# Sums of squares of the norms: elementwise adds on VectorE and GpSimd and one-column products instead of products with ones

## The chip, the cores and the metric

The kernel runs on one core of a Trainium2 chip. The metric is the device time of one execution in microseconds, from repeated runs. TensorE (PE in the profile; its weight loads are PEld) multiplies matrices into PSUM, VectorE (DVE), ScalarE (ACT) and GpSimd (POOL) work elementwise, and SyncE (SP) issues the transfers. Each engine takes its instructions in a fixed order and waits on semaphores for the others.

## What is computed

One inference step of a hybrid flow-matching model: two layers over 512 latent tokens and 128 context tokens of 1024 features, all in float32. A layer, cut to what matters here:

```python
def rmsnorm(x, g):
    y = x * rsqrt(mean(x * x, axis=-1, keepdims=True) + 1e-6)
    return y * g

h = rmsnorm(x, g_pre1) * (1 + scale1) + shift1
y = concat(diff_attention(h), gqa(h), ssd(h), s5(h)) @ w_out     # h @ w_in feeds all four
x = x + gate1 * rmsnorm(y, g_post1)
h = rmsnorm(x, g_pre2) * (1 + scale2) + shift2
g, v = split(dwconv(h @ w_up))
x = x + gate2 * rmsnorm((silu(g) * v) @ w_down, g_post2)
```

Every sub-block thus has a norm over 1024 features before and after it. The SSD mixer ends with a norm over 256 features, and queries and keys are normed over 64.

## The kernel before

Activations lie with features on the 128 partitions and tokens along the columns: a tensor of 1024 features is eight chunks of 128 x 642 (512 latent columns, two of padding, 128 context columns). The big products are done in float32 as three passes over a high and a low part of weights and activations (`lin3`, line 124), so a chunk of weights costs three instructions on TensorE per group of columns. Weights come through a pair of raw tiles `wr` (line 94); ScalarE casts the high part (line 103), VectorE and GpSimd take turns at the subtraction for the low part (line 106).

The tokens are worked in two groups, `SPANS` (line 48): columns 0 to 256 and 256 to 642. Around each norm the second group's products are meant to run on TensorE while the first group's norm is done. The functions that matter:

- `square` (line 305) is called once per chunk. ScalarE squares the chunk's columns into a tile `nsq` (line 311), and TensorE multiplies it by 32 columns of ones, which adds up the 128 features of the chunk (line 313). Chunk `c` writes into the quarter `c % 4` of the rows of a PSUM tile, so two chunks are added up in each quarter.
- `rstd` (line 315) is called once per group. ScalarE copies the four partial sums to `nsb` (line 322). For each tile of 128 tokens a one-column product with `sel4` adds the quarters and puts the tokens on the partitions (line 324). `rsqrt` (line 295) is one VectorE operation (line 300) and one power on GpSimd (line 302). A product with the identity broadcasts the factors over the partitions again (line 327).
- `prenorm` (line 334) makes the next activations from x (lines 345 to 353). `postnorm` (line 355) adds the normed y to x, chunk by chunk (VectorE line 365, then VectorE or GpSimd in turn, line 368), and calls `square` on the new x for the prenorm that follows.
- `norms` (line 375) ties the two: the first group's postnorm comes directly, its prenorm is kept back in `pending` until output tile `MID` = 6 of the second group is under way (`between`, line 387).

These norms are met at: the start (squares of x, `start`, line 1533 on); the output projection of each layer (squares of y in `put`, line 1601; of x in `postnorm`); the last block of the down projection of each layer (squares of y, line 1421; of x in `postnorm`, in layer 0 only, for layer 1's first norm). That makes 16 groups of eight squares. The SSD norm (line 1034 on) has two groups of two squares per layer. Behind the output projection come the first tiles of the up projection (`ffn_first`), behind layer 0's down projection the first tiles of layer 1's input projection (`first_proj`); both are worked group by group (`leading`, line 394).

The order of the instructions on an engine is not written by hand: a scheduler places them at build time by priorities (`prio`, with the numbers of `PR`, line 42) and by its own estimate of when things are ready. Tiles of a tag share their buffers: `nsq` has four for the first group, `nsr` two for the second (`NQ`, `NTMP`, lines 31 and 45).

Of the kernel before, what the change touches and what calls it, by code (L numbers as in the profile page):

```python
# [14 lines left out]
P = 128  # L15
# [15 lines left out]
NQ = (4, 2)  # L31
# [13 lines left out]
NTMP = (("nsq", SPLIT, NQ[0]), ("nsr", TW - SPLIT, NQ[1]))  # L45
# [23 lines left out]
for _n, _w in (("ident", 128), ("ones", 128), ("blk64", 2), ("su", 129), ("lt", 129),  # L69
               ("selc", 8), ("selh", 4), ("mhalf", 16), ("sel4", 1)):  # L70
    CST[_n] = (_o, _o + _w)
    _o += _w
# [3 lines left out]
class K:  # L76
# [10 lines left out]
    def load_w(self, src, nk, nm=128, keep=None, parts=None):  # L87
        """weights as (hi, lo) with hi + lo exact; they stay in the pool `keep` if one is given"""
# [20 lines left out]
    def load_w2(self, src, pool):  # L109
        """the same for 8 input chunks, as lists of their parts, in the place of hidden chunks"""  # L110
# [13 lines left out]
    def lin3(self, o, w, xs):  # L124
        """o = w^T x in three passes over the (hi, lo) parts"""
# [23 lines left out]
    def tri(self, lower, strict):  # L149
        """mask of the triangle of the rows not below (or not above) the columns"""  # L150
        o = int(strict == lower)
        return self.c("lt" if lower else "su")[:, o:o + 128]
# [13 lines left out]
    # exact-ish exponential on small tiles: returns (p, s), exp(x) = s * (1 + p)  # L166
# [30 lines left out]
    def cmul(self, pool, dre, dim, ar, ai, br, bi, nm, shp, e1=None, e2=None):  # L197
        """d = a * b on float planes (broadcast APs allowed)"""
# [17 lines left out]
    # ------------------------------------------------------------ adaLN  # L216
# [7 lines left out]
    def adaln(self, l, lo, hi, pool, banks="pp", bufs=2):  # L224
        """groups lo .. hi - 1 of 2048 columns of the modulation, in steps"""
# [16 lines left out]
    def adaln_end(self, l, g, parts, ps, pool, bank, sel, bufs):  # L242
        """column sums to the features on partitions; the 512s of a group lie in the order 0, 2, 1, 3"""
# [14 lines left out]
    def adaln_first(self, pool):  # L258
        """shift and scale of the first norm, half of the features after the other"""
# [12 lines left out]
    def gains(self, l, which):  # L272
        """(1 + scale) * g_pre, gate * g_post for sub-block `which` (0 mixer, 1 FFN)"""
# [20 lines left out]
    # ------------------------------------------------------------ norms  # L294
    def rsqrt(self, pool, ss, n, feats, tag):
        """(ss / feats + EPS) ** -0.5 on a small tile"""
# [8 lines left out]
    def square(self, pool, ps, gi, src, c, n=8, tmp=None):  # L305
        """adds src ** 2 over the features of chunk c of n for one group of tokens to the sums in ps (on the rows of a
        quarter, which depends on the chunk)"""
        t0, t1 = SPANS[gi]
        tmp = tmp or NTMP[gi]
        sq = pool.tile([P, tmp[1]], F32, tag=tmp[0], name="nsq", bufs=tmp[2])[:, :t1 - t0]  # L310
        self.nc.scalar.activation(sq, src[:, t0:t1], AF.Square)
        j = c % 4
        self.mm(ps[32 * j:32 * j + 32, 0:t1 - t0], self.c("ones")[:, 0:32], sq, c < 4, c >= n - 4)

    def rstd(self, pool, ps, gi, feats, tag="n", tmp=None):
        """per token 1 / rms from the sums in ps, on all partitions of ps; a function of the columns"""
        t0, t1 = SPANS[gi]
        tmp = tmp or NTMP[gi]
        n = len(LOC[gi])
        m = min(feats // 4, P)  # L320
        sb = pool.tile([P, tmp[1]], F32, tag=tmp[0], name="nsb", bufs=tmp[2])
        self.nc.scalar.copy(sb[0:m, 0:t1 - t0], ps[0:m, 0:t1 - t0])
        for j, c in enumerate(LOC[gi]):
            self.mm(ps[:, 400 + j:401 + j], sb[0:m, c - t0:c - t0 + 128], self.c("sel4")[0:m], True, True)
# [9 lines left out]
    def prenorm(self, pool, l, which, gi, acc):  # L334
        """h = rmsnorm(x) * (1 + scale) * g_pre + shift for one group of tokens"""
# [19 lines left out]
    def postnorm(self, pool, l, which, gi, acc, y, nacc, out=None):  # L355
        """x += gate * rmsnorm(y) * g_post for one group of tokens; nacc collects the squares of the new x"""
# [18 lines left out]
    def norms(self, pool, gi, st, y, post, pre, out=None):  # L375
        """from the sums of a group of tokens to the next activations; the end of the first group comes behind the
        start of the second one"""
        nacc = self.pss("ud"[gi])
# [8 lines left out]
    def between(self, m):  # L387
        """the rest of the first group's norms, once output tile MID of the second group is under way"""
# [4 lines left out]
    # ------------------------------------------------------------ input projection tiles  # L393
    def leading(self, jobs, bank, keep, wprio, place=None):
        """several output tiles, one group of the tokens after the other;
        jobs: (weights, put(first column, PSUM)), bank(i): PSUM tile"""
# [11 lines left out]
    def put(self, d, alt=0):  # L408
        """plain evacuation to the columns of a tile"""
# [10 lines left out]
    def dwconv(self, x, w, b, out):  # L420
        """centred depthwise conv of width 3 along the token axis"""
# [6 lines left out]
    def silu2(self, t, out, half):  # L428
        """out = silu(2 * half) by way of t"""
# [3 lines left out]
    def ysplit(self, c, src, scale=None):  # L433
        """mixer output chunk c (sample columns from 0, prompt columns at the end of src) to (hi, lo)"""
# [11 lines left out]
    # ------------------------------------------------------------ S5  # L446
    def first_proj(self, l, pb, lead):
        """inputs of the S5 mixer (columns ordered by position in the chunk of 8, chunk), first queries and keys,
        gates of the SSD"""
# [24 lines left out]
    def s5_tables(self, l, pool, bank="dd", wprio=None, bufs=1):  # L474
        """tables that depend on the parameters alone, to DRAM"""
# [17 lines left out]
        # step sizes, a_bar, input gain  # L493
# [56 lines left out]
        # powers a^0..a^8  # L550
# [6 lines left out]
        # unit phases e^{i theta 8 2^s}, decay |a|^8  # L557
# [13 lines left out]
        # powers per position in the chunk: into the states, out of the states  # L571
# [1205 lines left out]
```

## Time and profile before

| what | value |
|---|---|
| three runs | 2275.59, 2281.47, 2284.01 us; median 2281.47 |
| profiled execution | span 2270.7 us from the first to the last instruction, 32188 instructions |
| TensorE | busy 2064.1 us (91%), mean granted clock 0.930 of full |
| TensorE weight loads | 1692.5 us (75%) |
| VectorE | 1166.1 us (51%) |
| ScalarE | 728.5 us (32%) |
| GpSimd | 706.0 us (31%) |
| transfers | 232.19 MB, mean 102 GB/s |
| the chain that ended last | TensorE 75%, DMA 9%, VectorE 7%, GpSimd 3% |

The page gives the profiled execution's span and no device time of its own beside it; the runs' median lies 10.8 us above the span. Busy time of an engine is the time that its instructions took, with overlaps counted once. TensorE is pipelined: its instructions overlap, so the duration of one is longer than the time that it takes from its neighbours. The clock is granted at one of two levels, 1.2 or 2.4 GHz; 1.00 is the upper one throughout.

### The profile page before, as it was taken

The numbers are of one execution on the slowest core, as the hardware profiler recorded it, in microseconds if no ns is written. First come the engines' busy times: TensorE is split into PE (matmuls) and PEld (weight loads), VectorE is DVE, ScalarE is ACT, GpSimd is POOL, SyncE is SP. The second block draws the span as 40 slices with busy tenths as digits, with TensorE's granted clock in tenths as the row PEclk, the third lists the DMA queues.
The fourth block names the chain that finished last, engine by engine and source line by source line (L and its number), as shares of the span: only waits on it lengthen the run. The fifth ranks groups of instructions, "written<-read, shape, count | busy, mean of one in ns | idle before, by whom it ended". The sixth has DMA issues, their size and how long they took to land.

```text
span 2270.7 us, 32188 instructions
## 1 busy us (share of the span) xinstructions
PE 2064.1 (91%) x12698; PEld 1692.5 (75%) x12698; DVE 1166.1 (51%) x2376; ACT 728.5 (32%) x1256; POOL 706.0 (31%) x747
## 2 busy tenths in 40 slices
PE   5994988899999999999988889887989999999997
PEld 2884753454779788899976877655557899999985
DVE  7864874434558567233335358564565451323343
ACT  3421342232344223223324224343234443323231
POOL 4642523222232344122223324322233231212131
PEclk9996988889999999999998989888988999999998
DMA  7554324314313575422222542321022012222221
GB/s 285 165 179 135 121 68 124 93 49 142 108 38 108 166 247 186 131 82 63 84 77 77 174 131 90 111 67 49 11 65 94 19 47 84 70 80 68 82 75 47
DMA packets 95199, 232.19 MB, mean 102 GB/s; under 512 B 18120, under 2 KB 31816, under 8 KB 95048
## 3 DMA queue, kind: packets, MB, share of 16 engines
q1 hardware_dynamic: 95048, 230.14, 32.0%
q8 instruction: 100, 1.64, 0.3%
q14 instruction: 51, 0.42, 0.1%
HBM read 193.52 MB, written 36.58 MB: 101 GB/s over the span
## 4 chain that ended last, share of the span: by engine, by line
PE 75%; DMA 9%; DVE 7%; POOL 3%; issue 2%; ACT 2%; SPq 2%; POOLq 0%; DVEq 0%; ACTq 0%
PE psb L85 34%; PE psp L85 14%; PE pse L85 9%; PE psv L85 7%; PE psd L85 7%; PE psu L85 2%; DMA wm<-in_w_mod 1%; DMA ck<-in_cache_bk 1%; DMA ck<-in_cache_ak 1%; DMA wr<-in_w_down 1%; DMA s5yd<-s_u 1%; DMA wr<-in_w_out 1%; DMA s_tb<-s5td 1%; DMA s_u<-s5ud 1%; SPq L1160 1%
## 5 line engine op out<-in xcount | busy, mean ns | idle before, releaser
L85 PE MATMUL psb<-hh,wh 128*128 128x256 f32 (+1 forms) x1152 | 358.9, 312 | 2.3 <-DVE cv L425 2.3
L85 PE MATMUL psb<-hl,wh 128*128 128x256 f32 (+1 forms) x1152 | 357.9, 311 | 0.0
L85 PE MATMUL psb<-hh,wl 128*128 128x256 f32 (+1 forms) x1152 | 357.0, 310 | 0.0
L106 POOL TENSOR_TENSOR wl<-wr,wh 128x1024 fp32r<-128x1024 f32 (+3 forms) x83 | 181.6, 2188 | 449.5 <-ACT wh L103 427.1
L103 ACT CAST wh<-wr 128x1024 fp32r<-128x1024 f32 (+3 forms) x166 | 160.4, 966 | 427.9 <-PE psb L85 285.1
L85 PEld LDWEIGHTS psb<-hh,wh 128*128 128x128 f32 x1152 | 217.8, 189 | 13.2 <-issue 8.2
L85 PEld LDWEIGHTS psb<-hl,wh 128*128 128x128 f32 x1152 | 218.5, 190 | 3.4 <-issue 3.4
L85 PEld LDWEIGHTS psb<-hh,wl 128*128 128x128 f32 x1152 | 217.8, 189 | 3.4 <-issue 3.4
L85 PE MATMUL psp<-hh,wh 128*128 128x386 f32 (+1 forms) x544 | 182.2, 335 | 40.2 <-DVE dtr L839 13.1
L106 DVE TENSOR_TENSOR wl<-wr,wh 128x1024 fp32r<-128x1024 f32 (+3 forms) x83 | 95.2, 1147 | 184.5 <-ACT wh L103 184.0
L85 PE MATMUL psp<-hl,wh 128*128 128x386 f32 (+1 forms) x544 | 176.3, 324 | 1.5 <-DVE hl L353 1.4
L85 PE MATMUL psp<-hh,wl 128*128 128x256 f32 (+1 forms) x544 | 175.6, 324 | 0.0
L85 PE MATMUL psb<-uh,wh 128*128 128x256 f32 (+1 forms) x544 | 169.7, 312 | 0.0
L85 PE MATMUL psb<-ul,wh 128*128 128x256 f32 (+1 forms) x544 | 168.9, 310 | 0.0
L85 PE MATMUL psb<-uh,wl 128*128 128x256 f32 (+1 forms) x544 | 168.6, 310 | 0.0
L85 PEld LDWEIGHTS psp<-hh,wh 128*128 128x128 f32 x544 | 109.7, 202 | 52.8 <-DVE dtr L839 13.6
L85 PE MATMUL psv<-at_e,vt 128*64 128x512 f32 x240 | 136.3, 681 | 10.2 <-ACT at_e L1237 10.1
L1377 POOL TENSOR_TENSOR cv<-cv,cv 128x642 f32<-128x642 f32 x44 | 71.3, 1622 | 169.6 <-DVE cv L425 140.2
L85 PE MATMUL pse<-k,q 96*128 96x128 f32 (+5 forms) x288 | 100.2, 407 | 21.9 <-issue 6.7
L424 DVE SCALAR_TENSOR_TENSOR cv<-psb,vec,cv 128x641 f32<-128x641 f32 x72 | 63.4, 881 | 103.3 <-ACT cv L423 103.3
L85 PEld LDWEIGHTS pse<-k,q 96*128 96x128 f32 (+2 forms) x288 | 54.4, 205 | 79.0 <-issue 59.6
L85 PEld LDWEIGHTS psp<-hl,wh 128*128 128x128 f32 x544 | 109.5, 201 | 4.0 <-DVE hl L353 2.5
(497 smaller groups left out, 4596.5 us busy)
## 6 DMA issues: line engine op xcount, KB each, us to landing
wm<-in_w_mod SPq DMA_DIRECT2D x96, 512.0 KB
wr<-in_w_up SPq DMA_DIRECT2D x88, 512.0 KB
wr<-in_w_in SPq DMA_DIRECT2D x30, 512.0 KB
wr<-in_w_down SPq DMA_DIRECT2D x32, 384.0 KB
wr<-in_w_down SPq DMA_DIRECT2D x32, 320.0 KB
wr<-in_w_out SPq DMA_DIRECT2D x16, 512.0 KB
s_tb<-s5td SPq DMA_DIRECT2D x8, 992.0 KB
s_to<-s5td SPq DMA_DIRECT2D x8, 768.0 KB
```

What stands on the lines that cost most here:

```text
L85: self.nc.tensor.matmul(out, w, x, start=start, stop=stop)
L103: nc.scalar.copy(hv, rv)
L106: e.tensor_sub(lv, rv, hv.bitcast(F32))
L424: nc.vector.scalar_tensor_tensor(out[:, 1:TW], x[:, 0:TW - 1], w[:, 0:1], out[:, 1:TW], op0=ALU.mult, op1=ALU.add)
L1160: nc.sync.dma_start(k2[0:64, 0:TW].bitcast(F32), self.qd["bk"][0, r])
L1377: G.tensor_mul(cv[0], cv[0], cv[1])
```

## The change

The products with ones go. `square` still has ScalarE square each chunk. In a norm over 1024 features the squares of chunks 0 and 1 get tiles of their own (`na{gi}{c}`); those of chunks 2, 4 and 6 are added onto the first by VectorE, those of chunks 3 and 5 onto the second by GpSimd, and chunk 7 keeps its tile. `rstd` then has three tiles of squares (two in the SSD norm) and sums each over the features, with the tokens on the partitions, by a product of the tile as the stationary operand with one column of ones; three products are added up in PSUM per 128 tokens. The copy to `nsb` and the constant `sel4` are gone, as is the wait of `square` on PSUM. Both groups share the two buffers of `nsr` for chunks 2 to 7. The rest of the diff empties comments and docstrings.

```diff
-NQ = (4, 2)
-NTMP = (("nsq", SPLIT, NQ[0]), ("nsr", TW - SPLIT, NQ[1]))
+NTMP = (("nsr", TW - SPLIT, 2), ("nsr", TW - SPLIT, 2))
...
-               ("selc", 8), ("selh", 4), ("mhalf", 16), ("sel4", 1)):
+               ("selc", 8), ("selh", 4), ("mhalf", 16)):
...
-    def square(self, pool, ps, gi, src, c, n=8, tmp=None):
+    def sums(self, bank):
+        return self.pss(bank), {}
+
+    def square(self, pool, st, gi, src, c, n=8, tmp=None):
         t0, t1 = SPANS[gi]
-        tmp = tmp or NTMP[gi]
+        nc = self.nc
+        first = n == 8 and c < 2
+        tmp = (f"na{gi}{c}", t1 - t0, 1) if first else tmp or NTMP[gi]
         sq = pool.tile([P, tmp[1]], F32, tag=tmp[0], name="nsq", bufs=tmp[2])[:, :t1 - t0]
-        self.nc.scalar.activation(sq, src[:, t0:t1], AF.Square)
-        j = c % 4
-        self.mm(ps[32 * j:32 * j + 32, 0:t1 - t0], self.c("ones")[:, 0:32], sq, c < 4, c >= n - 4)
-
-    def rstd(self, pool, ps, gi, feats, tag="n", tmp=None):
+        nc.scalar.activation(sq, src[:, t0:t1], AF.Square)
+        if first or n < 8 or c == 7:
+            st[1][c] = sq
+        else:
+            a = st[1][c % 2]
+            (nc.gpsimd if c % 2 else nc.vector).tensor_add(a, a, sq)
+
+    def rstd(self, pool, st, gi, feats, tag="n"):
         t0, t1 = SPANS[gi]
-        tmp = tmp or NTMP[gi]
+        ps, sq = st[0], list(st[1].values())
         n = len(LOC[gi])
-        m = min(feats // 4, P)
-        sb = pool.tile([P, tmp[1]], F32, tag=tmp[0], name="nsb", bufs=tmp[2])
-        self.nc.scalar.copy(sb[0:m, 0:t1 - t0], ps[0:m, 0:t1 - t0])
         for j, c in enumerate(LOC[gi]):
-            self.mm(ps[:, 400 + j:401 + j], sb[0:m, c - t0:c - t0 + 128], self.c("sel4")[0:m], True, True)
+            for i, t in enumerate(sq):
+                self.mm(ps[:, 400 + j:401 + j], t[:, c - t0:c - t0 + 128], self.c("ones")[:, 0:1], i == 0,
+                        i == len(sq) - 1)
         r = self.rsqrt(pool, ps[:, 400:400 + n], n, feats, f"{tag}{gi}")
...
-        nacc = self.pss("ud"[gi])
+        nacc = self.sums("ud"[gi])
...
-            r = self.rstd(pool, ps, gi, 256, "sd", ("sd_ea", 512, 1))
+            r = self.rstd(pool, ps, gi, 256, "sd")
```

At the other places `self.pss(...)` becomes `self.sums(...)` in the same way.

## Rows read from the trace of the kernel before

**Rows 1.** Windows: stretch, length; PE, PEld, DVE, ACT, POOL busy; clock, DMA share, GB/s.
```profile
0.00:60.00 60.00, 33.15 (x230) 18.70 (x231) 43.22 (x201) 22.11 (x43) 26.79 (x56) 0.93 0.75 276
595.00:635.00 40.00, 39.92 (x221) 28.59 (x219) 16.94 (x34) 14.19 (x32) 8.53 (x7) 1.00 0.14 42
```

**Rows 2.** Windows of the tile of squares alone: PE, PEld, ACT busy (x instructions), clock, DMA.
```profile
595.00:631.00 36.00, 9.13 (x26) 1.78 (x26) 8.05 (x19) 1.00 0.14 45
631.00:636.00 5.00, 3.47 (x22) 1.11 (x22) 1.75 (x5) 1.00 0.28 97
645.00:675.00 30.00, 6.68 (x16) 1.10 (x16) 4.23 (x8) 0.99 0.02 6
1157.00:1210.00 53.00, 12.71 (x46) 2.63 (x46) 9.68 (x24) 0.94 0.15 50
1210.00:1232.00 22.00, 4.39 (x10) 0.69 (x10) 3.12 (x6) 0.84 0.48 139
```

**Rows 3.** Timeline of TensorE, last down projection: start, length, line, form, count.
```profile
2216.43 0.28 PE L85 MATMUL psb<-uh,kl 128*128 128x256 f32 x1
2216.64 0.62 PE L85 MATMUL psv<-nsq,cst 128*32 128x256 f32 x2
...
2217.41 0.28 PE L85 MATMUL psb<-ul,kh 128*128 128x256 f32 x1
2217.53 0.28 PE L85 MATMUL psb<-uh,kl 128*128 128x256 f32 x1
```

**Rows 4.** The same a little later, 386 columns.
```profile
2231.07 0.34 PE L85 MATMUL psb<-uh,kh 128*128 128x386 f32 x1
2231.34 0.84 PE L85 MATMUL psd<-nsq,cst 128*32 128x386 f32 x2
...
2232.39 0.34 PE L85 MATMUL psb<-uh,kl 128*128 128x386 f32 x1
```

**Rows 5.** Timeline of TensorE, layer 0: sums read by one-column products.
```profile
669.77 0.28 PE L85 MATMUL psp<-hh,kh 128*128 128x256 f32 x1
669.88 0.72 PE L85 MATMUL psd<-cst,nsb 128*128 128x1 f32 x6
...
670.67 0.28 PE L85 MATMUL psp<-hh,kl 128*128 128x256 f32 x1
```

**Rows 6.** Groups by form: busy us, mean ns of one, idle before.
```profile
L106 POOL TENSOR_TENSOR wl<-wr,wh 128x1024 fp32r<-128x1024 f32 x55 | 132.1, 2401 | 292.9 <-ACT wh L103 270.4 <-PE psv L85 22.4
...
L368 POOL TENSOR_TENSOR x<-x,nt 128x256 f32<-128x256 f32 x32 | 25.1, 783 | 38.1 <-DVE nt L365 37.6
...
L368 DVE TENSOR_TENSOR x<-x,nt 128x256 f32<-128x256 f32 x32 | 16.9, 544 | 0.0
```

**Rows 7.** Timeline of GpSimd, then of VectorE, before the last down projection.
```profile
2187.22 1.58 POOL L1377 TENSOR_TENSOR cv<-cv,cv 128x642 f32<-128x642 f32 x1 [2.94 <-DVE cv L425]
...
2187.98 1.50 DVE L106 TENSOR_TENSOR kl<-wr,kh 128x640 fp32r<-128x640 f32 x1 [0.91 <-ACT kh L103]
...
2193.18 0.82 DVE L106 TENSOR_TENSOR kl<-wr,kh 128x640 fp32r<-128x640 f32 x1 [0.24 <-ACT kh L103]
```

**Rows 8.** Timeline of TensorE, ScalarE, GpSimd, end of layer 0's output projection.
```profile
623.96 0.61 PE L85 MATMUL psv<-identr,rq_y 128*128 128x128 f32 x4
...
632.44 1.33 ACT L311 ACTIVATE nsq<-x 128x256 f32<-128x256 f32 x4
...
639.11 1.04 ACT L103 CAST kh<-wr 128x1024 fp32r<-128x1024 f32 x1 [1.29 <-DMA wr<-in_w_up]
...
632.61 2.97 POOL L106 TENSOR_TENSOR kl<-wr,kh 128x1024 fp32r<-128x1024 f32 x1 [2.64 <-ACT kh L103]
```

**Rows 9.** Timeline of VectorE, ScalarE, TensorE, end of layer 0's feed-forward.
```profile
1227.08 1.34 DVE L368 TENSOR_TENSOR x<-x,nt 128x256 f32<-128x256 f32 x2
...
1233.26 0.94 ACT L311 ACTIVATE nsq<-x 128x386 f32<-128x386 f32 x2 [1.20 <-PE psd L85]
...
1240.51 0.69 PE L85 MATMUL psp<-hh,wh 128*128 128x386 f32 x1 [1.41 <-ACT hh L348]
```

More of the change, by code (lines that the diff above doesn't have):

```diff
@@ L1035, in ssd @@
         for gi, (t0, t1) in enumerate(SPANS):
-            ps = self.pss("d")
+            ps = self.sums("d")
             for c in range(2):
                 self.square(pool, ps, gi, y[c], c, 2, (f"sd_ex{c}", 512, 1))
-            r = self.rstd(pool, ps, gi, 256, "sd", ("sd_ea", 512, 1))
+            r = self.rstd(pool, ps, gi, 256, "sd")
             for c in range(2):
@@ L1410, in ffn @@
                 for gi, (t0, t1) in enumerate(SPANS):
-                    st = self.pss("vd"[gi])
+                    st = self.sums("vd"[gi])
                     for m in range(8):
@@ L1552, in start @@
             for gi in range(2):
-                st = self.pss(SB[gi])
+                st = self.sums(SB[gi])
                 for c in range(8):
@@ L1597, in run @@
                             for gi, (t0, t1) in enumerate(SPANS):
-                                st = self.pss("vd"[gi])
+                                st = self.sums("vd"[gi])
                                 def put(m):
@@ L1714, in layout @@
     i = np.arange(P)
-    sel4 = np.zeros((P, 1), np.float32)
-    sel4[0::32] = 1
-    putc("sel4", sel4)
     putc("mhalf", np.full((P, 16), -0.5, np.float32))
```

## The prediction

> **What bounds the kernel now.** I read the busy times by stretch first. In the stretch of the mixer's output projection TensorE is busy 39.92 of 40.00 us at full clock, with the DMA engines at 0.14 and VectorE and GpSimd under half [rows 1]: whatever leaves TensorE's queue there shortens the stretch, as long as nothing else becomes late. At the start it is otherwise: 33.15 of 60.00 us, with DMA at 0.75 and 276 GB/s [rows 1], so the first norm waits for transfers.
>
> Next I asked where the products of the squares stand. A product of two float32 operands is two instructions on TensorE. In 595 to 631 us there are 26, that is 13 products: the first group's eight of y (256 columns) and five of the second group's eight (386). In 631 to 636 there are 11 products more, in 645 to 675 eight (x, second group), in 1157 to 1210 twenty-three, in 1210 to 1232 five [rows 2]. Layer 1 repeats this: 26 instructions in 1705 to 1741, 22 in 1741 to 1747, 16 in 1753 to 1786; the last feed-forward has 26 in 2205 to 2251.
>
> Then the timeline, for what one product costs. The duration of a pipelined instruction is no price; the shift of its neighbours is. A product of 256 columns sits between neighbours that start every 0.12 us: from 2216.43 to 2217.41 two starts of that pace and the product take 0.98, so the product costs 0.98 - 0.24 = 0.74 us [rows 3]. For 386 columns, with a pace of 0.12 x 386/256 = 0.18, it is 2232.39 - 2231.07 - 0.36 = 0.96 us [rows 4]. Where products stand together they overlap: eleven fill 3.47 us, 0.32 each [rows 2].
>
> **The change part by part.**
>
> *Squares' products removed.* A stretch with 13 costs 8 x 0.74 + 5 x 0.96 = 10.7 us; there are three (both output projections, the last down projection): 32.1. The eight of x behind each output projection: 2 x 7.7 = 15.4. In 1157 to 1210, 13 as above and ten bunched ones at 0.32: 13.9. The five behind it: 4.8. Sum 66.2 us.
>
> *One-column products added.* Three tiles of squares are now reduced per 128 tokens where one was. Six such instructions in the stream took 670.67 - 669.77 - 0.24 = 0.66 us, 0.11 each [rows 5]. A first group gets 8 instructions more (0.88), a second 12 (1.32). Four first groups of y and three second groups of x stand in the stream: 3.5 + 4.0 = 7.5 us. The other seven sums end a stretch. There 7.9 us come in (four times 1.32, three times 0.88); out go the two bunches of 3.47, the last products of the kernel and seven ScalarE copies with their hand-overs. I take 0, with -6 to +6 as bounds.
>
> *Elementwise adds.* Each norm over 1024 features gets three on VectorE and two on GpSimd. An add of 256 columns took 0.54 us on VectorE and 0.78 on GpSimd; for 386, scaled by columns, 0.82 and 1.18 at most [rows 6]. For y they come one per output tile, and a tile of the stream takes 15 products x 0.12 = 1.8 us or more, so I cost them at nothing; without that cover the last one costs at most 1.2. For x they stand behind VectorE's own work on x. There the bounds are 0 and 3 x 0.82 + 2 x 1.18 = 4.8 us per norm. For the second groups of x behind the output projections I take 0, because the eight stand in the next stage's stream [rows 2], which covers them. For the three first groups I take 2 each, nearer the low end, since only the last add of each engine is late: 6 us.
>
> *New waits.* A one-column product waits for the adds of both engines, and all of TensorE stands behind it (rival 5). A square now waits for the add that frees its buffer, two squares back, where it waited for a product; behind it ScalarE has casts and evacuations. An add of at most 1.18 us takes the place of a product of 0.96: nothing.
>
> *The lock.* One thing makes adds on two engines dearer than their rows. A VectorE subtraction of 640 columns took 1.50 us while GpSimd worked on two tensors, and 0.82 without [rows 7]: it ended as if it had waited for GpSimd to finish at 2188.80. The Trainium skill, page SBUF — State Buffer, section "Who interferes with whom", says that a VectorE instruction with two SBUF inputs and a GpSimd instruction that reads SBUF share a read port and that the later one stands still. The trace agrees (1.50 against 0.82 us); by the rule each of the new pairs would run one after the other, and the sum would go to the second rival's.
>
> *Cover lost.* The first group's chain has to run beside the second group's products. Its factors are broadcast at 623.96, its last squares start at 632.44 [rows 8]. Three of the five second-group products in that stretch lie behind 623.96. Shortening the stream there only uncovers the chain: 3 x 0.96 = 2.9 us lost in each of three places, 8.6 us. In the last feed-forward nothing waits for that chain, so nothing is lost.
>
> *The second group's squares of x.* At the end of layer 0's feed-forward the last x is written at 1228.42, yet ScalarE starts the last squares only at 1233.26, held by TensorE's product queue, and the first product of the projection on this group starts at 1240.51 [rows 9]. Without the products the squares follow x at once: 4.8 us come free, 2.0 go to 18 one-column instructions and 0.8 to an add: 2 us gained.
>
> *No change.* The start: its sums are ready before the modulation weights, at 276 GB/s [rows 1]; 0, between -2 and +3. The eight products of the SSD norms (four per layer): I take 0, since no row here shows an unbroken stream around them, with 8 x 0.96 = 7.7 as upper bound. No transfer moves and no other queue order is written by hand; priorities are kept, so the rest of the program should keep its order, with a few us either way.
>
> **Sum**: 66.2 - 7.5 - 6 - 8.6 + 2 = 46 us off the profiled span of 2270.7. The runs' median of 2281.47 is 10.8 us above that span, which I leave as it is: 2281.5 - 46.1 = 2235.4 us. A measurement of this kernel can tell about 0.5% from no change, 11.4 us.
>
> **The rivals.**
>
> 1. *Forecast: TensorE's stream sets the end and most of the removal is kept.* For it: 39.92 of 40.00 us busy [rows 1], and the shift of the neighbours [rows 3, 4]. Own range 2224 to 2250. Chance 0.50.
>
> 2. *The norm chain sets the end.* VectorE and GpSimd block each other over the new adds, and the whole second group's gain in the stream is uncovered: of 20 products, 19.2 us, another 10.6 are lost; the three first groups pay 4.8 instead of 2 (8.4); the 2 us of [rows 9] are not gained. 46 - 21 = 25 us: 2256. For it: 1.50 against 0.82 [rows 7]. Against: outside the last microseconds of a stretch both engines have room [rows 1]. Chance 0.20.
>
> 3. *More comes back.* The chain of the first group moves up with the stream and its adds hide: 8.6 and 6 us return, 61 in all: 2221; with the bound of the ends, 2215. For it: ScalarE loses copies that wait for TensorE, and squares that are held [rows 9]. Chance 0.15.
>
> 4. *The weights set the end, so that the change hardly does what it says.* Behind the output projection ScalarE's cast of the next weights at 639.11 waits for a transfer that waits for a buffer [rows 8]. If that chain binds at every such place, only the last feed-forward gains, 10.7 - 0.9 = 9.8: 2272, no change. Against: those buffers come free as the output projection proceeds, which itself moves up; DMA is at 0.14 [rows 1]. Chance 0.08.
>
> 5. *Slower: the sums wait behind GpSimd's weight subtractions.* The order on each engine is fixed beforehand. Where the adds of chunks 3 and 5 are queued behind the subtraction of a weight tile, 2.40 us on average [rows 6] and 2.97 just where the first group's sums end [rows 8], the one-column products hold up all that follows on TensorE. With two adds of 1.18 the price is 2.4 + 2.4 = 4.8 us, 14 norms (all but the two at the start): 67 us against 52 gained without the first groups' 6: 15 slower, 2296. It decides from 52/14 = 3.7 us per norm. Against: a subtraction is due only once per few us, and the sums of y have several us of slack. Chance 0.07.
>
> **How the numbers follow.** Faster by over 0.5% (below 2270) are cases 1 to 3: 0.85; case 4 is the same: 0.08; case 5 slower: 0.07. The range reaches from below case 3's middle with part of its bound (2213) to just above case 4 (2274): it leaves out case 5 and the far ends of 3.
>
> **What would show it.** In the new profile: TensorE's busy time down by tens of us and no 386-column products left on the squares' tiles; the output projection's stretch some 10 us shorter, with TensorE still busy throughout; a gap behind it not longer than now. The squares of x should follow VectorE directly, without waits for TensorE. If instead the one-column products show idle time ended by a GpSimd add, case 5 is at work; if TensorE's idle time behind the output projections grows by as much as the stream shrinks, case 2 or 4. The forecast is wrong if the mixers' attention and scan stretches, which the change leaves alone, move by more than 10 us, since then the new order of instructions and not the norms would make the difference.

## The result and the profile after

The change makes the kernel about 1% faster: 2254.98 us median (2250.08 to 2262.02) against 2280.09 (2275.59 to 2284.01), ratio 0.9896 with a 95% interval of 0.9878 to 0.9915. Run again (run 9 below) it gave 2253.19 against 2276.65, ratio 0.9892 [0.9873, 0.9911]. So 23 to 25 us are gained where 46 were forecast: the time lies in the range (2213 to 2274), above the likeliest case's own (2224 to 2250).

The page of the changed kernel, its busy times and the chain that ended last:

```profile
span 2256.4 us, 32073 instructions
...
PE 2010.0 (89%) x12606; PEld 1707.2 (76%) x12606; DVE 1200.6 (53%) x2424; ACT 720.4 (32%) x1236; POOL 735.8 (33%) x779
...
PE 68%; DVE 12%; DMA 11%; issue 3%; ACT 2%; POOL 2%; SPq 1%; POOLq 0%; ACTq 0%; DVEq 0%
```

TensorE lost 54 us of busy time (it had 2064.1) and the span only 14.3. Of the chain TensorE holds 68% where it held 75, VectorE 12% where it held 7. By these two executions, some 40 us of what TensorE no longer needs became idle time.

To see where, I cut the timelines at marks that both programs have: the first product on normalised activations, the first square of y behind each mixer, the first and last product of each feed-forward, the same for layer 1, and the end. Two executions of the kernel before (the second is the run "once more" below), two of the changed one, and two of the best version found (runs 7 and 11), in us:

| stretch | before | changed | best version |
|---|---|---|---|
| start, to the first product on activations | 41.7, 41.6 | 48.3, 47.7 | 41.9, 41.6 |
| layer 0's mixer | 554.3, 555.2 | 557.1, 556.0 | 551.8, 551.3 |
| its output projection, to the feed-forward's tiles | 114.7, 116.3 | 110.5, 110.7 | 103.1, 107.9 |
| feed-forward 0 | 496.4, 495.3 | 484.8, 484.6 | 485.6, 485.3 |
| turn to layer 1 | 7.3, 8.2 | 4.8, 4.4 | 4.4, 4.4 |
| layer 1's mixer | 492.6, 500.3 | 509.9, 507.5 | 499.8, 491.7 |
| its output projection | 115.1, 115.4 | 101.4, 104.0 | 99.6, 100.0 |
| feed-forward 1 | 428.8, 429.0 | 421.0, 419.5 | 420.6, 423.1 |
| rest | 19.7, 19.8 | 18.6, 19.4 | 18.2, 19.7 |

The forecast's sum, split over these places, is 11.3 us for each output projection, 13.6 for feed-forward 0 with the turn, and 9.8 for feed-forward 1 with the rest. Measured between the means of the pairs: 4.9 and 12.6, 14.3, and 9.4: 41.2 of 46.0. So the norms brought nearly what was forecast, save at layer 0's output projection. The rest went elsewhere: the start got 6.4 us longer and the two mixers 1.8 and 12.2, together 20.4. These were costed at nothing. (These four executions lie 20.8 us apart by their means, the medians 23 to 25.)

**The start.** VectorE and then TensorE around the first normalised activations (start, duration, line and shape; in brackets the idle time before). Kernel before:

```profile
15.60 0.17 DVE L194 SCALAR_TENSOR_TENSOR ea_st_e<-ea_st_z,ea_st_s 128x16 f32<-128x16 f32 x1
...
39.13 1.64 DVE L345 SCALAR_TENSOR_TENSOR nt<-x,gpre,psv 128x256 f32<-128x256 f32 x4
...
41.71 0.38 PE L85 MATMUL pse<-hh,wh 128*128 128x256 f32 x1
```

Changed kernel, VectorE, GpSimd and TensorE:

```profile
17.11 0.56 DVE L321 TENSOR_TENSOR nsq<-nsq 128x386 f32<-128x386 f32 x1 [1.07 <-ACT nsq L316]
...
19.65 0.98 DVE L193 SCALAR_TENSOR_TENSOR ea_st_e<-ea_st_z,ea_st_s 128x16 f32<-128x16 f32 x1
...
30.23 0.16 DVE L299 TENSOR_SCALAR rq_x<-psu 128x3 f32<-128x3 f32 x1 [1.73 <-PE psu L84]
...
47.26 1.64 DVE L352 SCALAR_TENSOR_TENSOR nt<-x,gpre,psv 128x256 f32<-128x256 f32 x4
...
18.52 2.08 POOL L321 TENSOR_TENSOR nsq<-nsq 128x386 f32<-128x386 f32 x1 [4.03 <-ACT nsq L316]
...
48.32 0.38 PE L84 MATMUL pse<-hh,wh 128*128 128x256 f32 x1 [0.49 <-ACT hh L355]
```

The sums themselves are early. What is late is VectorE, which in this stretch builds the scan's tables out of more than a hundred small operations in a row, and has the first `nt` queued behind them. Between these the build has put adds: they take 0.42 to 0.56 us each, VectorE waits for ScalarE's squares and for the one-column products (1.07 and 1.73), and a small operation beside a GpSimd add takes 0.98 us instead of 0.17. `nt` starts 8.1 us later, TensorE's first product 6.6.

**Layer 0's output projection.** Waits of TensorE from 605 to 660 us (total, times, longest), then VectorE, GpSimd and TensorE:

```profile
PE psu L84 <- DVE nsq L321: 6.4, 1, 6.4
PE psu L84 <- POOL rq_y L301: 3.9, 1, 3.9
```

```profile
633.95 2.56 DVE L375 TENSOR_TENSOR x<-x,nt 128x256 f32<-128x256 f32 x1
...
633.71 2.52 POOL L105 TENSOR_TENSOR kl<-wr,kh 128x1024 fp32r<-128x1024 f32 x1
636.18 0.90 POOL L321 TENSOR_TENSOR nsq<-nsq 128x256 f32<-128x256 f32 x1
...
639.46 2.72 PE L84 MATMUL psu<-cst,nsq 128*128 128x1 f32 x12 [6.37 <-DVE nsq L321]
```

This is the sequence that rival 5 described, at one place: a weight subtraction of 2.52 us stands on GpSimd among the first group's last adds. An addition of x that took 0.42 us at 629.23 lasts 2.56 beside it and ends 0.3 us behind it; the adds, the last squares (two buffers) and then TensorE queue up behind. The add that comes last is VectorE's, where rival 5 named GpSimd's. The Trainium skill, page SBUF — State Buffer, section "Who interferes with whom", has the later instruction of such a pair (VectorE with two inputs in SBUF, GpSimd reading SBUF) stand still until the earlier is done; this row agrees with it. The second execution shows the same wait, 6.4 us. In layer 1 the same wait is 1.1 us. All of TensorE's waits in the stretch together are 13.0 and 12.4 us in the two executions of the changed kernel, and 3.9 and 4.7 in those of before.

**Layer 1's mixer.** The change touches it only at its ends, but the order of its instructions is another one. Fifty microseconds of it, from 150 us behind its first product (elapsed; busy and count of TensorE, its weight loads, VectorE, ScalarE, GpSimd; clock, DMA share, GB/s). Kernel before, best version, changed kernel:

```profile
1364.40:1414.40 50.00, 49.07 (x309) 34.85 (x307) 40.79 (x65) 20.58 (x39) 24.31 (x34) 0.97 0.24 77
```

```profile
1336.90:1386.90 50.00, 48.87 (x276) 35.45 (x275) 34.91 (x56) 16.84 (x34) 21.95 (x33) 0.83 0.23 75
```

```profile
1355.50:1405.50 50.00, 42.76 (x280) 31.97 (x278) 31.19 (x50) 16.53 (x32) 15.95 (x21) 0.88 0.25 76
```

Two of TensorE's waits in the whole stretch, picked because they are longer in the changed kernel:

```profile
PE psd L84 <- DMA s_tb<-s5td: 12.4, 2, 6.7
...
PE psu L84 <- ACT q L1219: 7.1, 2, 6.1
```

and the first of them in the kernel before, which does not have the second:

```profile
PE psd L85 <- DMA s_tb<-s5td: 4.9, 1, 4.9
```

The wait for the scan's tables is 7.5 us longer, and a wait for q of some 6 us stands where TensorE was busy 49 of 50 us before. Neither line belongs to a norm over 1024 features. Other waits became shorter; all of TensorE's waits in the stretch together are 63.4 us in the kernel before and 79.9 in the changed one.

### The profile page after: what moved, and what is told of

Same layout as the page of the kernel before. It is cut to its first block, busy times and chain, and to the rows that moved or that the text cites. A ratio compares the mean times of both kernels' runs of the same rounds, so it can differ in the third digit from the quotient of the medians.

```text
span 2256.4 us, 32073 instructions
## 1 busy us (share of the span) xinstructions
PE 2010.0 (89%) x12606; PEld 1707.2 (76%) x12606; DVE 1200.6 (53%) x2424; ACT 720.4 (32%) x1236; POOL 735.8 (33%) x779
## 4 chain that ended last, share of the span: by engine, by line
PE 68%; DVE 12%; DMA 11%; issue 3%; ACT 2%; POOL 2%; SPq 1%; POOLq 0%; ACTq 0%; DVEq 0%
PE psb L84 34%; PE psp L84 10%; PE pse L84 9%; PE psv L84 6%; PE psd L84 6%; PE psu L84 2%; DMA wm<-in_w_mod 1%; DMA ck<-in_cache_ak 1%; DMA s_tb<-s5td 1%; DMA ck<-in_cache_bk 1%; DMA s5yd<-s_u 1%; DMA wr<-in_w_down 1%; DVE nt L372 1%; DVE x L375 1%; DMA wr<-in_w_out 0%
## 5 line engine op out<-in xcount | busy, mean ns | idle before, releaser
L84 PEld LDWEIGHTS psp<-hh,wh 128*128 128x128 f32 x544 | 108.4, 199 | 42.1 <-ACT y L1532 15.6
L84 PE MATMUL pse<-k,q 96*128 96x128 f32 (+5 forms) x288 | 97.5, 399 | 27.2 <-DMA k<-d_ak 10.1
L1198 DVE TENSOR_REDUCE mx<-pse 128x1 f32<-128x512 f32 x96 | 65.4, 687 | 104.2 <-PE pse L84 103.4
```

Source lines behind the costliest of these rows:

```text
L84: self.nc.tensor.matmul(out, w, x, start=start, stop=stop)
L1198: V.reduce_max(mx[:, m, qt:qt + 1], ps, axis=AX.X)
```

## The experiments

Three theories were to be told apart for the lost 20 us: the new order of the mixers, the new work of the start norm, and the new work of the SSD norms. Each version below keeps both forms of a norm and chooses per place (`True` or "old" is the form before, with products and `sel4`). For each the order of TensorE's instructions was compared with that of the two kernels.

**1. Start norm old.**

```diff
-                st = self.sums(SB[gi])
+                st = self.sums(SB[gi], True)
```

> Only the start norm goes back to sums by products; the SSD norms and the eight norms behind the projections stay as changed. As built, TensorE's order of instructions in layer 0's mixer (norms left out) agrees with that of before in 98 of 100 places (the changed kernel's in 74), and layer 1's mixer with that of the changed kernel in 91. Theory 1 (the new order of the untouched mixer work lost the time): the first square of layer 0's output projection comes at 596 us again (605.4 in the changed kernel), layer 1's mixer stays near the changed kernel's, time about 2246, 9 us under the changed kernel. Theory 2 (the SSD norms' own new work lost it): it stays near 605, time about 2255. Theory 3 (the start norm's own new work): 596 too, but then the gain stands already at 150 us, ahead of the attention and scan work.

2239.31 us, ratio 0.983 [0.9797, 0.9863]: 7 us below the 2246 of theory 1. First product at 40.9 us, layer 0's mixer takes 557.9 behind it, so the first square of y comes at 598.8. Its order is that of before, yet that mixer is no shorter than the changed kernel's; what was won stands ahead of it, as theory 3 says. The order counts at another place: the output projection behind it takes 105.0 instead of 110.5, with a wait of 0.8 us where 6.4 stood. Layer 1's mixer, in about the changed kernel's order, takes 506.0.

**2. Start and SSD norms new, the others old.**

```diff
-        nacc = self.sums("ud"[gi])
+        nacc = self.sums("ud"[gi], True)
...
-                    st = self.sums("vd"[gi])
+                    st = self.sums("vd"[gi], True)
...
-                                st = self.sums("vd"[gi])
+                                st = self.sums("vd"[gi], True)
```

> Start and SSD norms as changed, the eight norms behind the projections by products as before. As built, TensorE's order in layer 0's mixer is the changed kernel's (99 of 100), in layer 1's mixer that of before (99 of 100), though layer 1's SSD norm is new. Theory 1 (order): first square of layer 0's output projection at about 605, layer 1's stretch from the last product of layer 0's FFN to the first square of layer 1's output projection back at about 500 us (514.6 in the changed kernel); time about 2280 + 9 = 2289. Theory 2 (the SSD norms' own work): both stretches long, about 2280 + 24 = 2304. If neither, 2280.

2284.70 us, ratio 1.0028 [1.0007, 1.0048], nearest to theory 1's 2289. The start is late again (46.2), layer 0's mixer takes 559.7, layer 1's, in the order of before and with a new SSD norm, 498.7. The SSD norms' own work lengthens nothing there: theory 2 falls.

**3. All adds on GpSimd, and 4. all on VectorE.**

```diff
-            (nc.gpsimd if c % 2 else nc.vector).tensor_add(a, a, sq)
+            nc.gpsimd.tensor_add(a, a, sq)
...
+            nc.vector.tensor_add(a, a, sq)
```

(The first new line is run 3's, the second run 4's.)

> The whole change, but all adds of squares on GpSimd. As built, TensorE's order in the two mixers is that of before (98 and 96 of 100), while every norm keeps the new form. Theory 1 (order): both mixer stretches go back (596 and about 500 us), 24 us under the changed kernel, less what six GpSimd adds in a row cost at the projections' norms (0.7 to 1 us each, up to 3 us at each of three exposed places): 2231 to 2243. Theory 2 (the norms' own new work in the mixers): the stretches stay at 605 and 514 and the adds come on top: 2255 to 2265.

2250.73 us, ratio 0.9873 [0.9833, 0.9913], above the expected 2231 to 2243. Layer 1's mixer is back at 500.5. But the start is late (46.9) although layer 0's order is that of before, and layer 1's output projection takes 108.4 instead of 101.4. TensorE's wait there:

```profile
PE psu L84 <- POOL nsq L321: 5.6, 1, 5.6
```

This is rival 5 as it was stated: the last of these adds on GpSimd stands behind a weight subtraction of 2.35 us (1726.36) and takes 1.71 us (1728.66). In layer 0, where the adds are on GpSimd too, the same wait is 1.1 us.

> The whole change, but all adds of squares on VectorE. As built, TensorE's order in layer 0's mixer is close to the changed kernel's (96 of 100), in layer 1's mixer like neither (64 and 59). Theory of the lock and of GpSimd's queue at the norms: the wait of the one-column products behind layer 0's output projection (6.4 us in the changed kernel, behind an add held up by a weight subtraction on GpSimd) shrinks to 3 us or less and that stretch (596 to 711 in the kernel before) by about 4 us, the same in layer 1. Rival: VectorE is as late, since it also makes the new x, and the stretch stays within 1 us. Theory 1 (order) expects layer 0's mixer at about 605 and leaves layer 1's open; time 2240 to 2262.

2255.47 us, ratio 0.9907 [0.9873, 0.994], in the range. The theory of the lock missed: the wait did not shrink, and the stretch takes 109.5 us, about 1 us less, as its rival said. TensorE's wait there, and VectorE and GpSimd, in this version:

```profile
PE psu L84 <- DVE nsq L321: 6.8, 1, 6.8
```

```profile
636.19 3.42 DVE L321 TENSOR_TENSOR nsq<-nsq 128x256 f32<-128x256 f32 x2
...
636.82 2.52 POOL L105 TENSOR_TENSOR kl<-wr,kh 128x1024 fp32r<-128x1024 f32 x1
```

Now two adds of squares last 3.42 us beside the same subtraction. The engine of the adds is not the cause; the place of the subtraction is. Layer 1's mixer takes 508.0 in an order of its own.

**5. Run 1 with the start norm new again, its adds on GpSimd.** A third argument now names the engine of the adds: "g" for GpSimd alone, "s" split as in the change. With run 1 this is a pair with equal orders.

```diff
-                st = self.sums(SB[gi], True)
+                st = self.sums(SB[gi], False, "g")
```

> The run with the old start norm (2239), with the start norm new again but its adds all on GpSimd. As built, TensorE's order in both mixers is that of the run with the old start norm (100 of 100 places in each), so the two differ in the start norm alone. Theory A (the start norm's adds hold up VectorE's scan tables and with them the first activations): the first product on normalised activations comes at 46 to 47 us instead of 41, everything behind it is shifted by about that, time 2244 to 2246. Theory B (layer 0's mixer lost its time to the new order): time 2239 within 2.

2248.33 us, ratio 0.9863 [0.9836, 0.989], on another chip than run 1 and above the 2244 to 2246 expected; the medians differ by 9 us. VectorE and TensorE in this run, then in run 1:

```profile
45.64 1.64 DVE L352 SCALAR_TENSOR_TENSOR nt<-x,gpre,psv 128x256 f32<-128x256 f32 x4
...
46.70 0.58 PE L84 MATMUL pse<-hh,wh 128*128 128x256 f32 x1 [0.93 <-ACT hh L355]
```

```profile
38.89 1.64 DVE L371 SCALAR_TENSOR_TENSOR nt<-x,gpre,psv 128x256 f32<-128x256 f32 x4
...
40.93 0.38 PE L85 MATMUL pse<-hh,wh 128*128 128x256 f32 x1
```

Layer 0's mixer takes 556.9 against 557.9 and layer 1's 505.7 against 506.0: only the start differs, by 5.8 us (4.7 against run 10, the program of run 1 once more). Theory A holds: the start norm's adds cost this even when none of them stands in VectorE's queue. How they do it shows in VectorE's small operations. One of them in this run, the GpSimd adds beside it, and the same operation in run 1:

```profile
24.56 0.98 DVE L212 TENSOR_TENSOR s_xr<-cm_xsq,cm_xsq 128x16 f32<-128x16 f32 x1
...
23.52 1.98 POOL L321 TENSOR_TENSOR nsq<-nsq 128x386 f32<-128x386 f32 x2
```

```profile
22.01 0.17 DVE L213 TENSOR_TENSOR s_xr<-cm_xsq,cm_xsq 128x16 f32<-128x16 f32 x1
```

Eight operations ahead of `nt` last 0.66 to 1.01 us beside such an add, 5.6 us more in all than eight of 0.17. Over all fourteen executions the first product comes at 40.9 to 42.5 us with the old start norm and at 46.2 to 48.3 with the new one. Behind layer 0's output projection the subtraction now comes after the sums (TensorE's wait, GpSimd, TensorE):

```profile
PE psu L84 <- DVE nsq L321: 0.9, 1, 0.9
```

```profile
632.02 2.43 POOL L105 TENSOR_TENSOR kl<-wr,kh 128x1024 fp32r<-128x1024 f32 x1 [2.71 <-ACT kh L102]
...
630.27 1.50 PE L84 MATMUL psu<-cst,nsq 128*128 128x1 f32 x12 [0.90 <-DVE nsq L321]
```

The stretch takes 104.5 us, 6 less than in the changed kernel, with the same norm code; runs 1 and 10, in the same order, take 105.0 and 106.4. So that loss, 4 to 6 us, is the order's. It is not the 6.4 us of the one wait: all waits of TensorE in the stretch are 9.3 us here against 13.0, since the wait for the next activations is now the longer one (3.9 against 2.5), and the rest of the difference is busy time (95.2 against 97.5 us).

**6. Only the SSD norms new**, all others old: run 2 with the start norm old as well.

```diff
-                st = self.sums(SB[gi])
+                st = self.sums(SB[gi], True)
```

> The kernel before with the new form in the two SSD norms alone. As built, TensorE's order in layer 0's mixer is that of before (100 of 100), in layer 1's that of the run with the old start norm (96, against 70 with before). Theory of the order in layer 1: the stretch from its first product on the new activations to the first square of its output projection is 504 to 510 us as in the changed kernel (509.9) and the run with the old start norm (506.0), instead of 492.6 in the kernel before; time 2277 + 6 to 10. Rival (orders are worth the same, what differs is the spread of runs): 493 to 500, and time 2277 within 3. Layer 0's stretch of the same kind stays at 554 to 558 for both.

2293.59 us, ratio 1.0067 [1.0036, 1.0099], 12 us more. Layer 1's mixer takes 503.9, just short of the range expected. But layer 0's takes 566.3 in the order of before, against 554.3 and 555.2; the shift grows by some 5 us around 250 us and by 4 to 6 more around 380, where 50 us have a granted clock of 0.73 and before had 0.80. Both places lie ahead of the SSD norm. So only part of the 12 us is layer 1's order; why layer 0's mixer is longer stays open, with one trace.

**7. Start norm old, layer 0's adds on GpSimd, layer 1's split.**

```diff
-                st = self.sums(SB[gi])
+                st = self.sums(SB[gi], True)
...
-        nacc = self.sums("ud"[gi])
+        nacc = self.sums("ud"[gi], False, "gs"[post[0]])
...
-                    st = self.sums("vd"[gi])
+                    st = self.sums("vd"[gi], False, "gs"[l])
...
-                                st = self.sums("vd"[gi])
+                                st = self.sums("vd"[gi], False, "gs"[l])
```

> Start norm old, the other norms new, with the adds of layer 0 all on GpSimd and those of layer 1 split as in the change. As built, TensorE's order in both mixers is that of before (99 and 96 of 100). Theory of the order in layer 1: its mixer stretch is 494 to 501 us (506.0 in the run with the old start norm), its output projection's stretch stays at 100, while layer 0's costs some 3 us more and the turn between the layers 0.6 more; time 2234 to 2238. Rival (orders are worth the same): 2241 to 2244.

2232.66 us, ratio 0.9792 [0.9761, 0.9823]: the fastest so far, a little under the range expected. Layer 1's mixer is at 499.8. Layer 0's output projection costs nothing extra in this execution (103.1), but 107.9 in run 11, the same program: this stretch differs by 4.8 us between two executions.

**8. The kernel before once more.**

> The kernel before once more, to see how far the stretches of one program differ between two executions. If the differences between kernels of the same order are run to run: the first product of layer 0's mixer at 41.7 within 0.5, the projections' and FFN's stretches within 1 us, and the two mixer stretches (554.3 and 492.6) within 7 us, with the granted clock to match. If layer 1's comes out at 505 or more, the theory of the order falls.

2282.86 us. Start, output projections and feed-forwards repeat within 1.6 us, layer 1's mixer differs by 7.7 (500.3); both are a little more than expected. Much of the 7.7 arises in one stretch: the fifty microseconds shown above have a granted clock of 0.97 in the one execution and 0.83 in the other. So the first comparison of layer 1's mixers overstated the order's cost.

**9 to 12. Side by side on one chip**: the changed kernel; with the old start norm (run 1 again); run 7 again; and run 7 with the SSD norms old too. Only the last has an edit of its own:

```diff
-            ps = self.sums("d")
+            ps = self.sums("d", True)
...
-            r = self.rstd(pool, ps, gi, 256, "sd")
+            r = self.rstd(pool, ps, gi, 256, "sd", ("sd_ea", 512, 1))
```

> The changed kernel once more, on the same chip as the three kernels beside it. If its stretches repeat: first product of layer 0's mixer at 48.3 within 0.5, wait of the one-column products behind layer 0's output projection 5 to 7 us again and that stretch 110 within 1; layer 1's mixer 503 to 511 by the theory of the order (498 or less would speak for a mere spread). Ratio to before 0.988 to 0.991.

> The changed kernel with the old start norm, beside it on one chip. Earlier start (6.6 us), no wait behind layer 0's output projection (5.5 us), layer 1's mixer as in the changed kernel: 12 to 17 us under it, ratio to before 0.981 to 0.985.

> Start norm old, layer 0's adds on GpSimd, layer 1's split, beside the others on one chip. Theory of the order in layer 1: 5 to 9 us under the kernel with the old start norm alone, layer 1's mixer 494 to 501. Rival (its earlier median was a matter of the chip): within 2 us of it.

> The same kernel with the two SSD norms back to sums by products. As built, TensorE's order in layer 0's mixer stays that of before (99 of 100), in layer 1's mixer it is a new one (61 against before, 81 against the changed kernel). Theory of the order: layer 1's mixer 503 to 510 instead of about 500, 4 to 10 us slower than the kernel beside it. Rival (the SSD norms' new form is what lengthens the mixers): both mixers get shorter by 2 to 6 us and the kernel is faster than the one beside it.

| version | median us | ratio to before | layer 1's mixer |
|---|---|---|---|
| changed kernel | 2253.19 | 0.9892 [0.9873, 0.9911] | 507.5 |
| start norm old | 2241.65 | 0.9849 [0.9832, 0.9865] | 507.4 |
| run 7 | 2228.28 | 0.9796 [0.9774, 0.9819] | 491.7 |
| run 7, SSD norms old | 2233.15 | 0.9809 [0.9789, 0.9828] | 499.9 |

Run 9 repeats the changed kernel, its start 0.6 us early. The next two steps have the direction expected, not the size: 11.5 us for the start norm and what moves with it (12 to 17 expected), 13.4 more for the order and the engines (5 to 9 expected). The last misses in the mixer: its order of layer 1's mixer is neither kernel's, and at 499.9 it is not slow. So not every other order costs: of the two that are neither kernel's, this one is not slow and run 4's, with 508.0, is. Against run 7 the difference in time is unclear.

All executions of layer 1's mixer by order: in that of before 492.6, 500.3, 498.7, 500.5, 499.8, 491.7, mean 497.3, with both forms of the norms among them; in the changed kernel's or the one near it (run 1's, which agrees with it in 91 of 100 places; runs 5, 6 and 10 have run 1's in 96 or more) 509.9, 507.5, 506.0, 507.4, 505.7, 503.9, mean 506.7. They do not overlap; the order costs 9.4 us by the means. The waits part in the same way: TensorE waits for the scan's tables 4.7 to 5.3 us in the six short ones and 12.4 to 13.4 in the six long ones, and in all 63 to 68 us against 76 to 81. The granted clock does not: its mean over the stretch is 0.855 to 0.875 in the short ones and 0.868 to 0.873 in the long ones.

## Why the prediction was right or wrong

The time lies in the range, and in part by luck: the range took in the rivals' 2256 and 2272, whose mechanisms are not what set the time, and two terms put at nothing cost 20 us. By the prediction's own last sentence the forecast is wrong, since layer 1's mixer moved by 12.2 us between the pairs of executions above.

*TensorE's stream sets the end.* Right. Where the squares' products left the stream, the time came back nearly as summed (41.2 of 46.0 us; 47.1 in the best version, by the means of its two executions). That holds for the prices of 0.74 and 0.96 us from the shift of neighbours [rows 3, 4], whose sum is tested here as a whole and not one by one.

*"TensorE still busy throughout".* Wrong, though the stretch shortens as forecast. TensorE from 1715 to 1755 us in layer 1 of the changed kernel:

```profile
1715.00:1755.00 40.00, 34.03 (x209) 33.17 (x207) 31.35 (x54) 20.45 (x41) 19.69 (x17) 0.85 0.30 99
```

and the same forty microseconds of that layer in the kernel before:

```profile
1707.00:1747.00 40.00, 39.37 (x212) 28.07 (x212) 19.52 (x36) 16.80 (x35) 9.21 (x9) 1.00 0.20 67
```

Its waits in the changed kernel from 1715 to 1817:

```profile
PE psu L84 <- POOL rq_y L301: 3.4, 1, 3.4
PE psp L84 <- ACT hh L355: 1.8, 2, 1.5
PE psu L84 <- DVE nsq L321: 1.1, 1, 1.1
```

It is busy 34.03 of 40 us where it had 39.37. The first group's chain is uncovered there, at 6.3 us of waits where the kernel before has 4.2 in layer 1: 2.1 more, against 4.9 counted for cover and adds.

*"Three of the five second-group products in that stretch lie behind 623.96".* A misreading. The last three of the five in the kernel before:

```profile
620.97 0.83 PE L85 MATMUL psd<-nsq,cst 128*32 128x386 f32 x2
...
625.02 0.84 PE L85 MATMUL psd<-nsq,cst 128*32 128x386 f32 x2
...
628.29 0.84 PE L85 MATMUL psd<-nsq,cst 128*32 128x386 f32 x2
```

Two lie behind it, so the term is 5.8 us by its own rule and not 8.6, and the sum some 49 us. Measured with the adds, for which the sum has 4.9 us at each place, it is 2 us of waits more in layer 1; in layer 0 it is 5 in the order of before (9.2 to 9.3 in runs 1, 5 and 10, against 3.9 and 4.7) and 8 in the changed kernel's.

*One-column products, 0.11 us each* [rows 5]. Right at full clock; behind a gap they take twice that. Windows of the changed kernel: the idle gap behind layer 0's output projection, the twelve products that end it, and those around the twelve in layer 1, which stand below by themselves:

```profile
633.00:640.00 7.00, 0.63 (x4) 0.54 (x3) 5.93 (x7) 1.90 (x5) 4.09 (x3) 0.87 0.14 23
639.40:642.30 2.90, 2.72 (x12) 2.63 (x12) 0.01 (x1) 0.42 (x1) 0.00 (x0) 0.50 0.94 311
...
1726.00:1728.00 2.00, 2.00 (x17) 2.00 (x16) 1.24 (x3) 1.14 (x2) 0.00 (x0) 1.00 0.58 162
```

```profile
1726.16 1.39 PE L84 MATMUL psv<-cst,nsq 128*128 128x1 f32 x12
```

Twelve took 1.39 us at a granted clock of 1.00 and 2.72 at 0.50 (1.2 GHz), to which it had fallen after 6.4 us in which TensorE waited.

*The second group's squares of x.* Right. At the turn, 12.1 us lay between the end of the last x and the first product on that group (1228.42 to 1240.51 [rows 9]). In the changed kernel (VectorE, ScalarE, TensorE):

```profile
1223.56 1.09 DVE L375 TENSOR_TENSOR x<-x,nt 128x128 f32<-128x128 f32 x1
...
1224.75 0.94 ACT L316 ACTIVATE nsq<-x 128x386 f32<-128x386 f32 x2 [2.45 <-DVE x L375]
...
1225.92 4.00 PE L84 MATMUL psd<-cst,nsq 128*128 128x1 f32 x18 [5.11 <-DVE nsq L321]
...
1234.17 0.69 PE L84 MATMUL psp<-hh,wh 128*128 128x386 f32 x1 [1.41 <-ACT hh L355]
```

The squares follow x at once, and it is 9.5 us (1224.65 to 1234.17): 2.6 gained where 2 were forecast, although the 18 one-column products took 4.00 us and not 2.0 (at a granted clock of 0.50, behind 5.1 us of waiting). The sum counts these products twice, as 2.0 us here and as 1.3 of the 4.0 among the sums in the stream.

*The SSD norms: 0.* Right as far as can be told (run 2; runs 11 and 12, whose intervals overlap; what run 6's layer 0 lost lies mostly ahead of the SSD norm).

*"The start: its sums are ready before the modulation weights ... 0, between -2 and +3".* This step failed. I asked when the sums are needed and not what else VectorE and GpSimd do there. VectorE's tables set the time of the first activations, and the adds cost them 4.7 to 5.8 us (run 5 against runs 10 and 1) to 6.4 (the table), in run 5 because operations of 0.17 us last up to 1.01 beside a GpSimd add. The prediction had the lock among its terms, but only for the new adds against each other.

*"The rest of the program should keep its order, with a few us either way".* This step failed too, and the prediction had named it as what would make the forecast wrong: a mixer stretch moved by more than 10 us. The scheduler, which works with estimates of its own, gave both mixers another order. In layer 0's mixer that cost nothing that can be told from the spread (549 to 558 us in the order of before, and 566 in run 6; 556 to 562 in the changed kernel's; the means are 554 without run 6 and 559); in layer 1's 9.4 us, shown by the twelve executions; and behind layer 0's output projection 4 to 6 us, shown by runs 1, 5 and 10 against the changed kernel.

*The rivals.* The second gave 2256, close to the time measured, but not for its reason: the norms' places gained 41 us and not 25. The fifth's mechanism occurs once in the changed kernel, 6.4 us, and is dear there only together with the lock on VectorE that belonged to the second; run 3 shows it by itself, 5.6 us. The fourth was wrong: the places behind the output projections gained 17.5 us. (The range's lower end, 2213, is called part of the third's bound; all of it gives 2215.)

*The profiled span.* I left 10.8 us between span and median as they were. In the later runs the time lies 1.7 to 1.9 us above the span; the rest was the spread between executions of before, 2266.58 to 2291.43 us over the runs shown here.

## What to carry to other kernels

Cost a new elementwise step by what its engine has to deliver next at each place, not by when its own result is needed: at the start, ten adds beside a chain of small operations cost 5 to 6 us where the products had cost nothing that shows, and moving them all to GpSimd did not help, since most of them held up an operation of the chain. Where a scheduler makes the order at build time, compare the orders of the two programs before the times, and give the reordering a price of its own; versions whose orders agree are then the pairs from which a cost can be read. A single trace of a long stretch says little below its spread, here 8 us in 500; and one long wait is not the price of a stretch, since other waits grow where it goes.

## What was not expected of the hardware

Layer 1's mixer differs by 8 us between two executions of one program (of before, and of the best version), while the dense stretches of before repeat within 1.6; in the former the granted clock differs with it (0.97 and 0.83 in the same fifty microseconds). A wait of 6.4 us on TensorE doubled the price of the twelve products behind it, since the clock was then granted at 0.50. And a GpSimd subtraction of 2.52 us stretched what VectorE had with two tensors beside it: 2.56 instead of 0.42 us for one addition, 3.42 for two adds of squares. At the start a GpSimd add made operations of 16 columns, 0.17 us long, last up to 1.01.
